# Moving the small resident tiles of a two-layer float32r trunk into a pool of their own that ends on a multiple of 2 KB

## The chip, the cores and the metric

One core of one Trainium2 chip runs the kernel. The time is device microseconds of one execution of the program; several executions are timed, and the median counts. The engines work at the same time: TensorE (PE in the profile, PEld its weight loads), VectorE (DVE), ScalarE (ACT), GpSimd (POOL), SyncE (SP), which here issues all DMAs. The on-chip memory (SBUF) has 128 partitions; a tile takes the same byte addresses in each of them, so a tile's start is one number, in bytes of a partition.

## The reference

A trunk of two layers on 512 tokens of width 1024, all in float32. What matters here is what is multiplied:

```python
def swiglu(x, w_gu, w_down):                 # D_FF = 2816
    gate, up = jnp.split(x @ w_gu, 2, axis=-1)
    return (jax.nn.silu(gate) * up) @ w_down

# layer 0
x = x + 0.5 * swiglu(rms_norm(x, ffn1_norm[0]), ...)
h = rms_norm(x, mix_norm[0]) @ a_w_in[0]     # 6 gated DeltaNet heads, 4 heads over the memory
x = x + concat([o_a, o_m]) @ w_out[0]
x = x + 0.5 * swiglu(rms_norm(x, ffn2_norm[0]), ...)
# one latent K/V from x, shared by the next layer
# layer 1
x = x + 0.5 * swiglu(rms_norm(x, ffn1_norm[1]), ...)
h = rms_norm(x, mix_norm[1]) @ b_w_in[0]     # 6 MLA heads, 4 heads over the memory
x = x + concat([o_b, o_m]) @ w_out[1]
x = x + 0.5 * swiglu(rms_norm(x, ffn2_norm[1]), ...)
return rms_norm(x, final_norm)
```

## The kernel before

**How a product is made.** Activations lie feature-major: a tile of 128 features by 512 tokens. Each float32 operand is split exactly into a part that float32r holds and the remainder: xh and xl for the activations, gh and gl (or dh and dl) for the weights. `mm3` (L196 to L202) then makes three matmuls per 128 features: weights wh against xh (L200), wh against xl (L201), wl against xh (L202). The first operand after the output is the stationary one (128 columns, loaded by PEld), the second is streamed through it, 512 columns of 4 bytes, 2048 bytes of each partition.

**The work.** The four feed-forward parts (`ffn`, calls numbered 0 to 3) take most of the time. Each walks over 22 hidden tiles, two at a time: two tiles of up projection (`gemm`, twice 24 matmuls each: 8 chunks of features, 3 matmuls), whose results are normed, gated and split into hh and hl, and then the down projection (`down`) of the pair before, 8 output tiles of 6 matmuls each. So 96 up-projection matmuls (named mm in the profile, streaming nah, nal and the like, one letter per norm) are followed by 48 down-projection matmuls (dn, streaming hh and hl); at the border a few of the two kinds alternate. In the last pair of the last part (`finish`) the 512 tokens are done in two halves, with 256 columns. Between the parts stand mixer A (the DeltaNet heads in small 128-column float32 matmuls, with the next heads' projections, mm from nbh and nbl, beside them), the latent part, and mixer B. Both end in an output projection (wo, streaming oh and ol, which stand in the tiles of xh and xl). The memory's keys and values (memk, memv) are made inside the first feed-forward part and the latent part.

**What sets the order.** `Weights` loads 1 MB tiles (gr) by SP's queue, and splits them in pieces of 512 columns on ScalarE (L91, the float32r part) and VectorE (L92, the remainder), one to two tiles ahead of their use. The tile scheduler orders each engine's instructions from the program's order. Each engine runs its own list; semaphores join them.

**Where tiles stand.** A pool is one stretch of SBUF. Pools opened one after another follow each other, and in a pool each tag takes its buffers in the order of first use, each rounded up to a multiple of 32 bytes. The first free byte is 16512, which is 128 past a multiple of 2048. The pool `res` comes first, and in it, in this order: cst (the gains and other columns, 128x153, 640 bytes), x0 to x7 (2048 each), ident and ones (512 each), half and warm (32 each), the 16 tiles of xh and xl (2048 each), rcol (two columns of 4, 32 each), the two rows of reciprocal roots (2048 each), memc (32), memr and the memory's keys and values (1024 each), the squares and their sums (2048 each). The pool `wp` of the weight stream follows (gr, gh, gl, two buffers of 8192 bytes each), then the pools of the parts. So the small tiles decide where all later ones begin:

| tiles | start mod 2048 before | after |
|---|---|---|
| x0 to x7 | 768 | 0 |
| xh, xl (also oh, ol) | 1856 | 0 |
| gr, gh, gl | 928 | 1024 |
| feed-forward: g, u, hh, hl, dr, dh, dl | 928 | 1024 |
| latent ch, cl; mixer B's qh, ql | 928 | 1024 |
| memory mh, ml | 928, 1952 | 1024, 0 |
| ident, ones | 768, 1280 | 768, 1280 |

A matmul takes its 128 weight columns at multiples of 512 bytes from the start of gh, gl, dh or dl. Mixer A's own tiles have small ones among them and stand at many different starts, before and after.

The lines that the change and the prediction touch: the pools (L136 to L139), the constants (L180 to L189), `rstd_column` (L229 to L238), `memory_kv` (L373 to L377), `mm3` (L196 to L202), `Weights._split` (L91, L92).

Of the kernel before, what the change touches and what calls it, by code (L numbers as in the profile page):

```python
# [8 lines left out]
F32 = mybir.dt.float32  # L9
# [8 lines left out]
P = 128  # L18
# [17 lines left out]
NCOL = 0  # L36
# [20 lines left out]
class Weights:  # L57
    """A stream of weight tiles in the order of their use: raw loads run two tiles ahead,
    the exact split into a float32r part and the remainder runs one tile ahead."""

# [35 lines left out]
    def start(self, part, parts):  # L96
        """The first tile in parts: their loads, and later their splits by first()."""
        n = self.src[0].shape[1]
        if part == 0:
            t = self.pool.tile([P, self.size], F32, tag=self.tag + "r", bufs=self.raw_bufs,  # L100
                               name=f"{self.tag}r0")
            self.raws.append((t, n))
        c = slice(part * n // parts, (part + 1) * n // parts)
        self.nc.sync.dma_start(self.raws[0][0][:, c], self.src[0][:, c])
# [26 lines left out]
def trunk(ctx, tc, xT, memT, pos, cols, masks, wmem, wgu, wdn, wba, wain, wout, wdkv, wbin,  # L131
          wuqn, wuqr, wukn, wuv, outT, taps=None):
    nc = tc.nc
    taps = taps or {}

    res = ctx.enter_context(tc.tile_pool(name="res", bufs=1))  # L136
    wp = ctx.enter_context(tc.tile_pool(name="wp", bufs=1))
# [5 lines left out]
    def ps(tags, name):  # L143
        """A PSUM bank; "ab" takes the two pairs of banks by turns."""
        k = turn.get(tags, 0)
        turn[tags] = k + 1
        return pp.tile([P, S], F32, tag=tags[k % len(tags)], bufs=2, name=name)
# [31 lines left out]

# [1 line left out]
    cst = res.tile([P, NCOL], F32, name="cst")  # L181
    nc.sync.dma_start(cst, cols)
    x = [res.tile([P, S], F32, tag=f"x{c}", name=f"x{c}") for c in range(KD)]
    ident = res.tile([P, P], F32, name="ident")
    ones = res.tile([P, P], F32, name="ones")
    nc.vector.memset(ones, 1.0)
    half = res.tile([P, 8], F32, name="half")
    nc.vector.memset(half, -0.5)
    nc.scalar.copy(res.tile([P, 8], F32, name="warm"), half)  # L189

# [3 lines left out]

# [1 line left out]
    def mm3(out, ws, xs, first=True, last=True):  # L196
# [20 lines left out]
    def rsqrt(out, src, scale):  # L217
        """(src * scale + eps) ** -0.5 of a few columns."""
        nc.vector.tensor_scalar(out, src, scale, EPS, op0=ALU.mult, op1=ALU.add)
        nc.gpsimd.tensor_tensor(out, out, half[:, :out.shape[1]], op=ALU.pow)  # L220

    def rows_of(c, n, name, tags="d"):
        """Token columns c [128, n] as one row in every partition, in PSUM."""
        p = ps(tags, name)
        for i in range(n):
            nc.tensor.transpose(p[:, i * P:(i + 1) * P], c[:, i:i + 1].broadcast_to([P, P]), ident)
        return p

    def rstd_column(pool, parts, scale, tag, n=NB):  # L229
        """1/rms over the features of parts (squares, feature-major), token-major."""  # L230
        p = ps("d", tag + "ss")
        for i in range(n):
            for j, a in enumerate(parts):
                nc.tensor.matmul(p[:, i:i + 1], a[:, i * P:(i + 1) * P], ones[:, 0:1],
                                 start=j == 0, stop=j == len(parts) - 1)
        c = pool.tile([P, n], F32, tag="rcol", bufs=2, name=tag + "c")
        rsqrt(c, p[:, :n], scale)
        return c  # L238

    def rstd_rows(pool, c, tag, n=NB):  # L240
        """The same in every partition."""
        pr = rows_of(c, n, tag + "row")
        r = pool.tile([P, n * P], F32, tag="rstd", bufs=2, name=tag + "r")
        nc.scalar.copy(r, pr[:, :n * P])
        return r

    class Norm:
        """x * gain split for the tensor engine, chunk by chunk; 1/rms follows once all are in."""

# [103 lines left out]

# [1 line left out]
    memk, memv, memr = [], [], []  # L355

    def memory_kv(l, hook=None):
        with tc.tile_pool(name=f"mem{l}", bufs=1) as mp:
# [14 lines left out]
            if l == 0:  # L373
                c = res.tile([P, 2], F32, name="memc")
                r = res.tile([P, 256], F32, name="memr")
                nc.vector.tensor_copy(c, rstd_column(mp, [acc], 1.0 / 1024, "mem", 2))
                nc.scalar.copy(r, rows_of(c, 2, "memrow")[:, :256])  # L377
                memr.extend((c, r))
            c, r = memr
# [22 lines left out]
    def memory_attention(l, q, pool, out, ts="ab", tt="d", to="c"):  # L402
        """q: two tiles of two heads each, feature-major; out(pair, psum) takes the result."""
        for pr in range(2):
# [43 lines left out]
    def out_begin(os, order, held):  # L448
        """The first four tiles of the output projection without the last operand."""
        for _ in range(2):  # L450
# [21 lines left out]

# [1 line left out]
    def mixer_a(norm, nxt):  # L474
        with ExitStack() as st:
# [25 lines left out]
            def project(h):  # L501
                """q, k, v after their convolutions and the gate, feature-major."""
                o = []
# [24 lines left out]

            # decay and write strength of every head, by rows
            w = G.get()  # L530
# [45 lines left out]
            def prepare(h, q, k, v, gs):  # L576
                """Everything of a head that does not wait for the scan."""
                bb, Gb = t("bb"), t("Gb")
# [3 lines left out]
                cs = [slice(n * P, (n + 1) * P) for n in range(NB)]  # L582
                # decay between tokens, transposed: rows j, columns i
                Dm = t("Dm")
# [7 lines left out]
                nc.scalar.activation(kf, kf, AF.Exp)  # L592
                # lengths of k and q, from their token-major forms; they enter as factors of what
                # the products of the raw k and q are multiplied with
                ss = ap.tile([P, 8], F32, tag="ss", bufs=3, name="ss")
                pkt, pqt = ps("b", "kt"), ps("b", "qt")
                for i, (a, p) in enumerate(((k, pkt), (q, pqt))):
# [6 lines left out]
                    yield  # L604
                # k k^T and k q^T within a block
                pk = ps("b", "kk")
# [16 lines left out]
                nc.vector.tensor_mul(bb, bb, eG)  # L623
                AT = Db  # its upper triangle and diagonal are never read
                nc.vector.tensor_mul(AT, pk, Db)
                # (I + A)^-1: small diagonal blocks by substitution, rows of A brought to every
                # partition of their block
                tmp = t("tmp")
# [45 lines left out]
            def scan(h, AT, xt, QK, kd, vb, qd, kb, fin, rq, gs):  # L674
                cs = [slice(n * P, (n + 1) * P) for n in range(NB)]
                nb = P // SUB
                # the inverse goes on by doubling the size of its blocks; two units by turns
                X, Z = [], []
# [20 lines left out]
                for s in LEVELS:  # L699
# [11 lines left out]
                    for g in range(2):  # L711
                        pr = ps("c", "r")
                        # the last step needs of X the first blocks of 64 only
                        w = 64 if s == LEVELS[-1] else P
# [11 lines left out]
                for g in range(2):  # L726
# [14 lines left out]
                    yield  # L741
                # scan over the blocks, the output token-major
                po = ps("c", "o")
# [54 lines left out]
            def drive(*tasks):  # L798
                """Emit the tasks (a generator and about how many steps it has) side by side, so
                that the products of one fill the waits of the others; return what they return."""  # L800
                done = [0.0] * len(tasks)
# [51 lines left out]

# [1 line left out]
    def rope_tables(cs, sn):  # L855
# [30 lines left out]
    def latent_norm(pool, src, gain, hi, lo):  # L886
        """rms norm over two feature tiles, split for the tensor engine; in two steps."""
        sqs = []
# [27 lines left out]
    def norm_project(norm, w, out):  # L916
        """The first products of a norm, two tiles of features."""
        p0 = gemm(norm, w, 256, 0)
# [5 lines left out]

# [1 line left out]
    def mixer_b(norm, lat, nxt):  # L926
        with ExitStack() as st:
            bp = st.enter_context(tc.tile_pool(name="mixb", bufs=1))

            # tags of the squares of a norm, free meanwhile  # L930
            lent = {"cq": "sq", "qraw": "sq", "qn": "sqa"}
# [86 lines left out]

            # one head begins when the one before it is half done
            tasks = [head(h) for h in range(NH)]  # L1020
# [11 lines left out]

# [1 line left out]
    def gain(name, l=0):  # L1034
# [51 lines left out]
    def finish(ws, hs, pool):  # L1086
        """The last products and the final norm by halves of the tokens, the norm of the first
        half beside the products of the second."""
        acc, rc = [None, None], [None, None]
# [150 lines left out]
```

## Time and profile before

| | us |
|---|---|
| median of three runs | 2081.82 |
| the three runs | 2086.16, 2081.36, 2081.82 |
| span of the profiled execution (first to last instruction) | 2085.2 |
| TensorE busy in the span | 2038.2 |

The profile is of one execution. Its span, 2085.2 us, is the time from its first to its last instruction; the time of a run counts a little more around it (of the three, 2086.16 us lies nearest). Times in the rows are microseconds from the start of the span. Matmuls are pipelined: a row's length is longer than the step to the next row's start, and the steps between starts tell how fast TensorE goes.

### The profile page before, as it was taken

How to read it: one execution, taken by the hardware profiler on the slowest of the kernel's cores; microseconds unless marked ns; L12 is line 12 of the kernel's file. 1: busy time of each engine (PE TensorE's matmuls, PEld its weight loads, DVE VectorE, ACT ScalarE, POOL GpSimd, SP SyncE). 2: the span in 40 equal slices, each digit the busy share in tenths (PEclk: the TensorE clock that was granted, in tenths of full speed). 3: DMA queues.
4: the chain of work that ended last, by engine and by line, in shares of the span. 5: the costliest groups of instructions: out<-in, count | busy, mean ns of one | idle time of the engine just before them, and what ended most of it. 6: DMA issues, size and time to landing. Idle time of an engine off the chain costs nothing.

```text
span 2085.2 us, 24007 instructions
## 1 busy us (share of the span) xinstructions
PE 2038.2 (98%) x9264; PEld 1617.9 (78%) x9264; DVE 1239.3 (59%) x2311; ACT 750.0 (36%) x1566; POOL 118.0 (6%) x85
## 2 busy tenths in 40 slices
PE   8999999989999999999999999999999999999998
PEld 6888888777777678888888888888875588888886
DVE  7655555777777595555547655555557554555555
ACT  6332222565664353222225422222243343222221
POOL 1000000200100020000002000000020020000001
PEclk9999999999999999999999999999999999999999
DMA  6332222332222132322222422222111132222211
GB/s 235 111 118 84 101 82 74 114 112 62 68 91 71 54 125 101 101 84 98 102 71 76 173 101 81 101 93 91 62 39 49 61 124 98 82 100 101 98 44 41
DMA packets 43642, 191.59 MB, mean 92 GB/s; under 512 B 5756, under 2 KB 10108, under 8 KB 28808
## 3 DMA queue, kind: packets, MB, share of 16 engines
q1 hardware_dynamic: 43528, 190.05, 26.6%
q8 instruction: 73, 1.20, 0.2%
q14 instruction: 41, 0.34, 0.0%
HBM read 184.57 MB, written 4.42 MB: 91 GB/s over the span
## 4 chain that ended last, share of the span: by engine, by line
PE 50%; issue 35%; DVE 7%; DMA 3%; ACT 2%; POOL 2%; SPq 0%; DVEq 0%; POOLq 0%; ACTq 0%
PE mm L201 9%; PE mm L202 9%; PE mm L200 9%; PE dn L200 4%; PE dn L201 4%; PE dn L202 4%; DMA ab<-sub 2%; PE wo L200 1%; PE wo L202 1%; PE wo L201 1%; PE sc L995 1%; PE sc L994 1%; DVE gl L92 1%; PE bo L1015 1%; POOL nfsa L269 1%
## 5 line engine op out<-in xcount | busy, mean ns | idle before, releaser
L91 ACT CAST gh<-gr 128x512 fp32r<-128x512 f32 x474 | 261.3, 617 | 380.8 <-PE mm L201 356.1
L92 DVE TENSOR_TENSOR gl<-gr,gh 128x512 fp32r<-128x512 f32 x474 | 314.3, 689 | 15.9 <-ACT gh L91 9.6
L337 DVE SCALAR_TENSOR_TENSOR x<-dn,x 128x512 f32<-128x512 f32 x344 | 236.4, 688 | 89.9 <-PE dn L202 88.3
L200 PE MATMUL dn<-hh,dh 128*128 128x512 f32 (+1 forms) x720 | 278.9, 387 | 1.4 <-DVE x L337 1.0
L202 PE MATMUL dn<-hh,dl 128*128 128x512 f32 (+1 forms) x720 | 277.8, 386 | 0.0
L201 PE MATMUL dn<-hl,dh 128*128 128x512 f32 (+1 forms) x720 | 277.8, 386 | 0.0
L91 ACT CAST dh<-dr 128x512 fp32r<-128x512 f32 x176 | 96.6, 617 | 296.9 <-PE dn L201 284.9
L304 ACT ACTIVATE g<-g 128x512 f32<-128x512 f32 x88 | 55.5, 632 | 323.3 <-DVE g L303 323.2
L200 PEld LDWEIGHTS dn<-hh,dh 128*128 128x128 f32 x720 | 135.3, 188 | 34.9 <-DVE x L337 6.2
L202 PEld LDWEIGHTS dn<-hh,dl 128*128 128x128 f32 x720 | 135.3, 188 | 27.4
L201 PEld LDWEIGHTS dn<-hl,dh 128*128 128x128 f32 x720 | 135.5, 188 | 27.0
L200 PE MATMUL mm<-nah,gh 128*128 128x512 f32 x352 | 140.7, 401 | 6.2 <-ACT gh L116 5.9
L201 PE MATMUL mm<-ncl,gh 128*128 128x512 f32 x352 | 140.3, 399 | 2.0 <-DVE ncl L214 2.0
L201 PE MATMUL mm<-nal,gh 128*128 128x512 f32 x352 | 140.8, 400 | 0.4 <-DVE nal L214 0.4
L202 PE MATMUL mm<-nah,gl 128*128 128x512 f32 x352 | 140.6, 399 | 0.6 <-DVE gl L117 0.6
L200 PE MATMUL mm<-nch,gh 128*128 128x512 f32 x352 | 140.4, 399 | 0.0
L202 PE MATMUL mm<-nch,gl 128*128 128x512 f32 x352 | 140.2, 398 | 0.0
L200 PE MATMUL mm<-ngh,gh 128*128 128x512 f32 x352 | 139.7, 397 | 0.0
L201 PE MATMUL mm<-nel,gh 128*128 128x512 f32 x352 | 139.6, 397 | 0.0
L201 PE MATMUL mm<-ngl,gh 128*128 128x512 f32 x352 | 139.6, 397 | 0.0
L202 PE MATMUL mm<-neh,gl 128*128 128x512 f32 x352 | 139.6, 397 | 0.0
L200 PE MATMUL mm<-neh,gh 128*128 128x512 f32 x352 | 139.6, 396 | 0.0
(414 smaller groups left out, 3566.6 us busy)
## 6 DMA issues: line engine op xcount, KB each, us to landing
gr<-wgu SPq DMA_DIRECT2D x87, 1024.0 KB, 4.8
dr<-wdn SPq DMA_DIRECT2D x88, 512.0 KB, 4.0
gr<-wain SPq DMA_DIRECT2D x13, 1024.0 KB, 4.8
gr<-wout SPq DMA_DIRECT2D x8, 1024.0 KB, 5.9
gr<-wmem SPq DMA_DIRECT2D x4, 1024.0 KB, 4.8
ab<-sub SPq DMA_DIRECT2D x6, 512.0 KB
x<-xT SPq DMA_DIRECT2D x8, 256.0 KB, 6.9
mt<-memT SPq DMA_DIRECT2D x16, 128.0 KB, 2.4
```

Source lines behind the costliest of these rows:

```text
L91: nc.scalar.copy(hi[:, a:b], raw[:, a:b])
L92: nc.vector.tensor_sub(lo[:, a:b], raw[:, a:b], hi[:, a:b].bitcast(F32))
L200: nc.tensor.matmul(out, wh, xh, start=first and k == 0, stop=False)
L201: nc.tensor.matmul(out, wh, xl, start=False, stop=False)
L202: nc.tensor.matmul(out, wl, xh, start=False, stop=last and k == n - 1)
L269: nc.gpsimd.tensor_tensor(acc, self.acc, sq, op=ALU.add)
L304: nc.scalar.activation(g, g, AF.Silu)
L337: nc.vector.scalar_tensor_tensor(x[m], p, 0.5, x[m], op0=ALU.mult, op1=ALU.add)
L994: nc.tensor.matmul(p[:, :nk], qn[:, c], kn[:, :nk], start=True, stop=False)
L995: nc.tensor.matmul(p[:, :nk], qr[h // 2][rows, c], lat["kr"][rows, :nk], start=False, stop=False)
L1015: nc.tensor.matmul(po[:, b * P:], vv[b][:, h * P:(h + 1) * P], pt[:, b, b * P:], start=b == 0, stop=b == NB - 1)
```

## The change

A new pool `small` is opened ahead of `res` and takes cst, ident, ones, half, warm, the columns of reciprocal roots (rcol, from whichever part asks for one) and memc. A tile of 24 zeros (fill, 96 bytes) fills it up: 640 + 512 + 512 + 32 + 32 + 96 + 64 + 32 = 1920 bytes, from 16512 to 18432 = 9 x 2048. In `res` only tiles of 2048 and 1024 bytes remain. The diff without the lines that only delete comments and docstrings:

```diff
+    small = ctx.enter_context(tc.tile_pool(name="small", bufs=1))
     res = ctx.enter_context(tc.tile_pool(name="res", bufs=1))
     wp = ctx.enter_context(tc.tile_pool(name="wp", bufs=1))
...
-    cst = res.tile([P, NCOL], F32, name="cst")
+    cst = small.tile([P, NCOL], F32, name="cst")
     nc.sync.dma_start(cst, cols)
     x = [res.tile([P, S], F32, tag=f"x{c}", name=f"x{c}") for c in range(KD)]
-    ident = res.tile([P, P], F32, name="ident")
-    ones = res.tile([P, P], F32, name="ones")
+    ident = small.tile([P, P], F32, name="ident")
+    ones = small.tile([P, P], F32, name="ones")
     nc.vector.memset(ones, 1.0)
-    half = res.tile([P, 8], F32, name="half")
+    half = small.tile([P, 8], F32, name="half")
     nc.vector.memset(half, -0.5)
-    nc.scalar.copy(res.tile([P, 8], F32, name="warm"), half)
+    nc.scalar.copy(small.tile([P, 8], F32, name="warm"), half)
+    nc.vector.memset(small.tile([P, 24], F32, name="fill"), 0.0)
...
     def rstd_column(pool, parts, scale, tag, n=NB):
...
-        c = pool.tile([P, n], F32, tag="rcol", bufs=2, name=tag + "c")
+        c = small.tile([P, n], F32, tag="rcol", bufs=2, name=tag + "c")
...
             if l == 0:
-                c = res.tile([P, 2], F32, name="memc")
+                c = small.tile([P, 2], F32, name="memc")
```

The order of instructions stays the same on TensorE, ScalarE, GpSimd and SP. On VectorE one is added at the start of the program, where the constants are set and the first chunks of x are split (nal is the remainder of a chunk of x, gl that of the first weight tile). Before:

```order
L186 MEMSET ones 128x128
L188 MEMSET half 128x8
L214 SCALAR_TENSOR_TENSOR nal_101<-x_68,cst,nah_100 128x512
L117 TENSOR_TENSOR gl_105<-gr_84,gh_104 128x512
L214 SCALAR_TENSOR_TENSOR nal_111<-x_69,cst,nah_110 128x512
L214 SCALAR_TENSOR_TENSOR nal_117<-x_70,cst,nah_116 128x512
```

With the change, where lines are numbered two or three higher:

```order
L188 MEMSET ones 128x128
L190 MEMSET half 128x8
L192 MEMSET fill 128x24
L217 SCALAR_TENSOR_TENSOR nal_106<-x_71,cst,nah_105 128x512
L117 TENSOR_TENSOR gl_110<-gr_89,gh_109 128x512
L217 SCALAR_TENSOR_TENSOR nal_116<-x_72,cst,nah_115 128x512
L217 SCALAR_TENSOR_TENSOR nal_122<-x_73,cst,nah_121 128x512
```

The zeros of fill have come in third; all that follows keeps its order.

## Rows read from the trace of the kernel before

**Rows 1.** Page, busy us (share of the span) and instructions of each engine.
```profile
PE 2038.2 (98%) x9264; PEld 1617.9 (78%) x9264; DVE 1239.3 (59%) x2311; ACT 750.0 (36%) x1566; POOL 118.0 (6%) x85
```

**Rows 2.** Windows: us; PE, PEld, DVE, ACT, POOL busy (x instructions); clock, DMA share, GB/s.
```profile
500.00:600.00 100.00, 93.27 (x558) 74.17 (x557) 76.03 (x233) 63.27 (x196) 13.77 (x8) 1.00 0.23 75
900.00:1000.00 100.00, 100.00 (x432) 81.06 (x432) 52.81 (x85) 26.77 (x48) 0.00 (x0) 1.00 0.27 95
2038.50:2050.50 12.00, 12.00 (x53) 9.66 (x52) 2.76 (x4) 1.25 (x2) 0.00 (x0) 1.00 0.00 1
2050.81:2061.47 10.66, 10.66 (x48) 8.83 (x47) 6.74 (x10) 0.62 (x1) 0.00 (x0) 1.00 0.00 0
```

**Rows 3.** Page, chain that ended last, shares by engine.
```profile
PE 50%; issue 35%; DVE 7%; DMA 3%; ACT 2%; POOL 2%; SPq 0%; DVEq 0%; POOLq 0%; ACTq 0%
```

**Rows 4.** Timeline of TensorE (start us, length us): 93 up projections, first and last.
```profile
1209.31 0.40 PE L200 MATMUL mm<-neh,gh 128*128 128x512 f32 x1
...
1230.86 0.40 PE L202 MATMUL mm<-neh,gl 128*128 128x512 f32 x1
```

**Rows 5.** Timeline of TensorE: 48 down projections, then 48 of half width, firsts and lasts.
```profile
2050.81 0.39 PE L200 MATMUL dn<-hh,dh 128*128 128x512 f32 x1
...
2061.47 0.39 PE L202 MATMUL dn<-hh,dl 128*128 128x512 f32 x1
2061.70 0.28 PE L200 MATMUL dn<-hh,dh 128*128 128x256 f32 x1
...
2067.33 0.28 PE L202 MATMUL dn<-hh,dl 128*128 128x256 f32 x1
```

**Rows 6.** Timeline of TensorE: down projections behind two up projections.
```profile
1954.85 0.40 PE L201 MATMUL mm<-ngl,gh 128*128 128x512 f32 x1
1955.08 0.39 PE L202 MATMUL mm<-ngh,gl 128*128 128x512 f32 x1
1955.32 0.40 PE L200 MATMUL dn<-hh,dh 128*128 128x512 f32 x1
...
1957.40 0.39 PE L200 MATMUL dn<-hh,dh 128*128 128x512 f32 x1
```

**Rows 7.** Groups by shape: names, xcount | busy us, mean ns of one | idle before.
```profile
L200 PE MATMUL mm<-nch,gh 128*128 128x512 f32 x352 | 140.4, 399 | 0.0
...
L200 PE MATMUL dn<-hh,dh 128*128 128x512 f32 x688 | 269.8, 392 | 1.4 <-DVE x L337 1.0
...
L200 PE MATMUL mm<-nbh,gh 128*128 128x512 f32 x208 | 87.9, 422 | 0.3 <-DVE cp L517 0.3
...
L200 PE MATMUL wo<-oh,gh 128*128 128x512 f32 x128 | 51.4, 408 | 0.9 <-ACT oh L210 0.8
...
L200 PE MATMUL memk<-mh,gh 128*128 128x256 f32 x32 | 9.3, 291 | 0.0
...
L200 PE MATMUL dn<-hh,dh 128*128 128x256 f32 x32 | 9.1, 285 | 0.0
```

**Rows 8.** Groups by shape, VectorE.
```profile
L92 DVE TENSOR_TENSOR gl<-gr,gh 128x512 fp32r<-128x512 f32 x473 | 313.9, 690 | 15.9 <-ACT gh L91 9.6 <-PE nfrow L226 5.9
...
L337 DVE SCALAR_TENSOR_TENSOR x<-dn,x 128x512 f32<-128x512 f32 x344 | 236.4, 688 | 89.9 <-PE dn L202 88.3
...
L211 DVE TENSOR_TENSOR hl<-u,hh 128x512 fp32r<-128x512 f32 x88 | 60.2, 685 | 3.4 <-ACT hh L210 3.2
```

**Rows 9.** Timeline of VectorE, the first 5 us.
```profile
0.95 0.07 DVE L188 MEMSET half<- 128x8 f32 x1
4.82 0.75 DVE L214 SCALAR_TENSOR_TENSOR nal<-x,cst,nah 128x512 fp32r<-128x512 f32 x1 [3.81 <-ACT nah L213]
```

**Rows 10.** Page, DMA issues: out<-in, count, KB each, median us to landing.
```profile
gr<-wgu SPq DMA_DIRECT2D x87, 1024.0 KB, 4.8
```

**Rows 11.** Timeline of TensorE: mixer A's 24 matmuls with 64 weight columns, first and last.
```profile
395.09 0.39 PE L200 MATMUL mm<-nbh,gh 128*64 128x512 f32 x1
...
400.41 0.39 PE L202 MATMUL mm<-nbh,gl 128*64 128x512 f32 x1
```

## The prediction

> **What bounds the kernel now.** I read the busy times first. TensorE is busy 98% of a span of 2085.2 us, VectorE 59% [rows 1]. [...] The chain that ended last says the same: TensorE's work and its "issue" (waiting for nothing that the profile shows) make up 85% of it, VectorE 7%, DMA 3% [rows 3]. So over four fifths of the kernel the time is the number of matmuls times the spacing of their starts. [...]
>
> **The spacing, by tile.** In the timeline of TensorE, 93 up-projection matmuls in a row start between 1209.31 and 1230.86 us, 92 steps: 21.55 / 92 = 234.2 ns, though each row is 0.40 us long [rows 4]. The last 48 full-width down-projection matmuls start between 2050.81 and 2061.47: 10.66 / 47 = 226.8 ns [rows 5]. Both stream 512 columns of float32r past 128 weight columns. [...] Other traffic does not separate the two kinds: from 2038.5 to 2050.5 us only up projections run, DMA is at 0.00 and VectorE at 23%; from 2050.81 the down projections follow with VectorE at 63%, and they are the faster ones [rows 2].
>
> What differs is the start address of the streamed operand. By the sizes of the tiles, xh and xl begin at 1856 mod 2048, which is 64 mod 128; hh, hl (and ch, qh) begin at 928 mod 2048, which is 32 mod 128, as do all the weights. So the fast kind has stream and weights at the same place mod 512 (416 both), the slow kind has them 96 bytes apart (320 against 416). The output projection streams oh and ol from the tiles of xh and xl; it is on the slow side.
>
> There is also a transient. Where two up-projection matmuls have come between down projections, the nine steps after them, from 1955.32 to 1957.40 us, take 2.08 us, 231 ns each, though all nine stream and load at the down projection's addresses [rows 6]. Such transients follow every mix of the two kinds; spread over all down projections I put them at 1.3 ns, 228.1 on average instead of 226.8 (an estimate: a dozen or so of 48 come about 5 ns late).
>
> **The change, part by part.**
> (1) xh and xl move to 0 mod 2048, weights and feed-forward tiles to 1024 mod 2048. Stream and weights are now at the same place mod 512 everywhere. The nearest measured case with this property is the down projection, so I take its 226.8 ns for every 128x512 float32r matmul.
> Feed-forward up projections: 352 x 3 x 4 = 4224 one group of the twelve, [rows 7], each 234.2 - 226.8 = 7.4 ns: 31.3 us, all on the path, as TensorE has no idle time there [rows 2].
> Down projections: 688 x 3 = 2064 [rows 7], from 228.1 to 226.8: 1.3 x 2064 = 2.7 us.
> Mixers and the latent part: 208 x 3 of mixer A's projection, 24 with 64 weight columns, 128 x 3 of the output projections [rows 7], and 168 in the inputs of the latent part and mixer B (groups like these), together 1200 x 7.4 = 8.9 us. In mixer A TensorE is 93% busy and also waits for VectorE and ScalarE [rows 2], so I count two thirds: 5.9 us; bounds 0 and 8.9.
> Sum: 31.3 + 2.7 + 5.9 = 39.9 us.
> [...] I take 226.8 because it is the only spacing that rows show for the equal-place case.
> (2) VectorE, ScalarE, POOL: the remainders of the weights work on three tiles at 928 mod 2048 (690 ns), the update of x on a tile at 768 and a PSUM bank (688), the remainder of u at 928 (685) [rows 8]. Different starts, one price: I count nothing for moving them, either way; if they changed by 1% they would hide behind TensorE in the feed-forward stretches, where VectorE has 47% to spare.
> (3) The new VectorE instruction, 128x24 zeros: the 128x8 one took 0.07 us at 0.95 us, and VectorE then sits idle for 3.81 us until ScalarE's first result [rows 9]. The zeros fall into that pause. Nothing; if that cover were gone, 0.07 us.
> (4) The two buffers of the reciprocal roots are now shared with the memory part's column, which had its own. The users lie tens of microseconds apart, and the order of instructions is the same on every engine. Nothing.
> (5) DMA: a 1 MB weight tile lands 4.8 us after its issue [rows 10] and one is needed every 11 us of up projection. A start at 1024 instead of 928 can change a little of 4.8; hidden.
> If matmuls come sooner, the next late thing would be VectorE, whose share would go from 53 to 55%. It stays hidden.
>
> The profiled execution spans 2085.2 us and took about 1 us more (2086.16 is the nearest of the three times): 2086.2 - 39.9 = 2046.3. The same 39.9 off the median of 2081.8 gives 2041.9, **2042 us**. With the mixers' bounds and a spacing of 226 to 228 ns the case's own range is 2034 to 2052.
>
> [...]
>
> **The rivals.**
> [...]
> 2. *Slower: a start on a multiple of 64 is the bad one.* The slow kind starts at 0 mod 64, the fast ones at 32 mod 64, and after the change every stream starts at 0 mod 64. Then the up projections stay at 234.2 and the down projections go there: 2064 x 6.1 = 12.6 us, and 312 of half width x 7.5 = 2.4: 2097 us. It counts as slower once the down projections exceed 231 ns (3 x 2064 = 6.2 us, 0.3%). Against it: in [rows 6] matmuls at 32 mod 64 take 231 ns too.
> 3. *No difference*: the surplus hangs on something that comes with xh and xl (sums over 24 matmuls instead of 6; their place low in the memory), and addresses mod 2048 don't matter. 2078 to 2085. [...]
>
> **How the numbers follow.** Forecast 0.42, rival 1 0.30, rival 2 0.13, rival 3 0.15. A measurement of this kernel tells 0.3% (6 us) from nothing, so faster is 0.72, same 0.15, slower 0.13. From 1960 to 2087 lie the forecast, rival 3 and the larger part of rival 1 (0.24): 0.81.
>
> **What would show it.** In the profile after: a run of 92 steps of up projection takes 20.9 us instead of 21.55; 441 matmuls in 100 us instead of 432; no transients after a mix; VectorE rows unchanged at 685 to 690 ns. [...] The forecast is wrong as well if TensorE gains and idle time for VectorE or a lower granted clock eats it.

## The result, and the profile after

The changed kernel takes 2046.32 us (median of four runs, 2043.36 to 2050.37) against 2082.14 us for the kernel before (four runs): a ratio of 0.9821, 95% interval 0.9803 to 0.9839, or 35.8 us less. The prediction was 2042 (1960 to 2087). The profiled execution spans 2045.2 us and took 2047.07; that of before spans 2085.2.

The page of the changed kernel, busy time of each engine, beside [rows 1]:

```profile
PE 1998.0 (98%) x9264; PEld 1612.7 (79%) x9264; DVE 1238.8 (61%) x2312; ACT 749.9 (37%) x1566; POOL 118.3 (6%) x85
```

TensorE still has the same 9264 matmuls and is still busy 98% of the span, but the busy time itself fell by 40.2 us. The other engines do what they did (VectorE 1238.8 against 1239.3 us). So the gain is in the matmuls.

The windows of the changed kernel, the same stretch of 900 to 1000 us as in [rows 2], and the last 48 full-width down projections:

```profile
900.00:1000.00 100.00, 100.00 (x443) 82.71 (x442) 53.12 (x85) 27.38 (x49) 0.00 (x0) 1.00 0.29 99
2010.90:2021.56 10.66, 10.66 (x49) 8.82 (x47) 6.74 (x10) 0.62 (x1) 0.00 (x0) 1.00 0.00 0
```

443 matmuls instead of 432 in 100 us, both at a granted clock of 1.00. The down projections take 10.66 us as before.

The timeline of TensorE in the changed kernel: the same 93 up projections as in [rows 4], first and last.

```profile
1189.03 0.39 PE L203 MATMUL mm<-neh,gh 128*128 128x512 f32 x1
...
1209.88 0.39 PE L205 MATMUL mm<-neh,gl 128*128 128x512 f32 x1
```

20.85 / 92 = 226.6 ns a step, against 234.2. That is the down projection's spacing of [rows 5] (226.8; a hundredth of a microsecond in the starts is 0.1 to 0.2 ns a step).

The same two up projections with ten down projections behind them as in [rows 6], in the changed kernel's timeline:

```profile
1917.40 0.40 PE L205 MATMUL mm<-ngh,gl 128*128 128x512 f32 x1
1917.64 0.40 PE L203 MATMUL dn<-hh,dh 128*128 128x512 f32 x1
...
1919.72 0.39 PE L203 MATMUL dn<-hh,dh 128*128 128x512 f32 x1
```

The nine steps from 1917.64 to 1919.72 take 2.08 us, as before. This transient did not go away. Others did: of 75 places where six or more steps between down projections follow an up projection without a stall, the first six average above 229 ns in 36 before and in 17 with the change.

VectorE's groups by shape and its first two small fills, beside [rows 8] and [rows 9]:

```profile
L92 DVE TENSOR_TENSOR gl<-gr,gh 128x512 fp32r<-128x512 f32 x473 | 314.9, 693 | 15.9 <-ACT gh L91 9.8 <-PE nfrow L229 5.8
L340 DVE SCALAR_TENSOR_TENSOR x<-dn,x 128x512 f32<-128x512 f32 x344 | 236.9, 689 | 89.1 <-PE dn L205 88.0
...
L214 DVE TENSOR_TENSOR hl<-u,hh 128x512 fp32r<-128x512 f32 x88 | 60.7, 689 | 3.1 <-ACT hh L213 2.9
```

```profile
0.95 0.07 DVE L190 MEMSET half<- 128x8 f32 x1
0.97 0.08 DVE L192 MEMSET fill<- 128x24 f32 x1
```

The prices are within 4 ns of those before (690, 688, 685), though all these tiles moved. The new fill of 0.08 us lies in the pause before the first chunk of x.

**Where the 40 us went**, from the starts of each part's first matmul in the two timelines:

| part | before, us | after, us | less |
|---|---|---|---|
| feed-forward part 0, with the memory's keys and values | 389.22 | 381.59 | 7.63 |
| mixer A | 277.10 | 274.04 | 3.06 |
| its output projection, to the start of part 1 | 74.08 | 73.19 | 0.89 |
| feed-forward part 1 | 374.17 | 367.03 | 7.14 |
| latent part | 32.25 | 31.97 | 0.28 |
| feed-forward part 2 | 368.83 | 360.66 | 8.17 |
| mixer B | 131.66 | 128.11 | 3.55 |
| its output projection, to the start of part 3 | 50.48 | 49.23 | 1.25 |
| feed-forward part 3, to the end | 381.55 | 373.34 | 8.21 |

Most of one of these lines is not the change's. In mixer B the two profiles differ by 3.1 us in one place, and there the granted clock differs. Windows of 5 us of the kernel before:

```profile
1615.00:1620.00 5.00, 4.46 (x18) 1.94 (x14) 1.96 (x6) 2.32 (x6) 0.00 (x0) 1.00 0.00 0
1620.00:1625.00 5.00, 5.00 (x13) 2.41 (x13) 1.79 (x6) 0.56 (x2) 0.00 (x0) 0.52 0.00 0
1625.00:1630.00 5.00, 5.00 (x20) 3.60 (x20) 2.37 (x10) 1.42 (x4) 0.00 (x0) 0.80 0.00 0
```

The same place in the changed kernel:

```profile
1588.00:1593.00 5.00, 4.46 (x18) 2.15 (x16) 2.11 (x7) 2.31 (x6) 0.00 (x0) 1.00 0.00 0
1593.00:1598.00 5.00, 5.00 (x20) 2.77 (x20) 3.11 (x13) 1.23 (x4) 0.00 (x0) 1.00 0.00 0
```

In both TensorE idles 0.54 us in the first window; in the profile of before the granted clock is then 0.52 and 0.80 in the next two windows, and in that of the changed kernel it stays at 1.00. The 68 matmuls of this stretch take 21.26 us with the drop and 18.13 to 18.15 without. Of the thirteen profiles of this study four have the drop (before, the two runs below that put pads by part, and the one that starts from the kernel before), nine don't. The up projection steps at 234, 227, 229 to 233 and 227 ns in these four, so the drop goes with no one spacing, and the same 0.54 us of idle time stands in all thirteen. One profile of each kernel can't show whether the drop comes with an execution; but over 27 timed runs of the kernel before, the mean granted clock goes from 0.990 (2089.45 us) to 0.997 (2078.07 us), so something of this kind differs between runs of one kernel. Without it the two profiles are 36.9 us apart, which agrees with the medians' 35.8.

### The profile page after: what moved, and what is told of

It reads as the page before. It is cut to its first block, busy times and chain, and to the rows that moved or that the text cites. A ratio compares the mean times of both kernels' runs of the same rounds, so it can differ in the third digit from the quotient of the medians.

```text
span 2045.2 us, 24008 instructions
## 1 busy us (share of the span) xinstructions
PE 1998.0 (98%) x9264; PEld 1612.7 (79%) x9264; DVE 1238.8 (61%) x2312; ACT 749.9 (37%) x1566; POOL 118.3 (6%) x85
## 4 chain that ended last, share of the span: by engine, by line
PE 50%; issue 36%; DVE 7%; DMA 3%; ACT 2%; POOL 2%; SPq 0%; DVEq 0%; POOLq 0%; ACTq 0%
PE mm L204 9%; PE mm L205 9%; PE mm L203 9%; PE dn L203 4%; PE dn L204 4%; PE dn L205 4%; DMA ab<-sub 2%; PE wo L203 1%; PE wo L205 1%; PE wo L204 1%; PE sc L998 1%; PE sc L997 1%; PE bo L1018 1%; DVE gl L92 1%; POOL nfsa L272 1%
## 5 line engine op out<-in xcount | busy, mean ns | idle before, releaser
L205 PE MATMUL mm<-ngh,gl 128*128 128x512 f32 x352 | 137.0, 389 | 0.0
```

The source lines that it names most:

```text
L205: nc.tensor.matmul(out, wl, xh, start=False, stop=last and k == n - 1)
```

## The experiments

Each kernel but the last is the changed kernel with the edit shown. Each ratio is to the kernel before as timed beside that run (medians from 2081.21 to 2084.36 us). Difference means the start of the streamed operand minus the start of the weights. In all of them a step is the distance of two starts in TensorE's timeline, over the same 93 up projections as above (92 steps) unless the text says otherwise.

**Absolute or relative place: four runs.** The forecast said that stream and weights must stand at the same place; rival 1 said that a misaligned stream pays by itself, whatever the weights do. In the changed kernel both begin at 0 mod 128. The edits move one of the two, by the length of fill and by an idle tile ahead of the weights' pool:

```diff
-    nc.vector.memset(small.tile([P, 24], F32, name="fill"), 0.0)
+    nc.vector.memset(small.tile([P, FILL], F32, name="fill"), 0.0)
+    gap = ctx.enter_context(tc.tile_pool(name="gap", bufs=1))
     wp = ctx.enter_context(tc.tile_pool(name="wp", bufs=1))
+    nc.vector.memset(gap.tile([P, GAP], F32, name="step"), 0.0)
```

FILL, GAP are 24, 8 (weights moved by 32 bytes), 40, 16 (stream by 64, weights by 128), 24, 16 (weights by 64), 32, 24 (stream by 32, weights by 128).

> The stream (xh, xl) stays at 0 mod 128, weights and feed-forward tiles go to 32 mod 128. Three theories, each for the up projection (stream 0, weights 32) and the down projection (32, 32). R, relative place: stream and weights must begin at the same place mod 128: up projection back to 234 ns, down projection 226.8, about 2085 us. S, the stream alone decides (0 and 32 mod 128 cheap, 64 dear): both 226.8 ns, 2046 us. W, weights on a multiple of 64 bytes are cheap with any stream, off it only a stream at the same place is: up projection 234 ns, about 2085 us, as R.

> The stream goes to 64 mod 128, weights and feed-forward tiles stay at 0 mod 128. R, same place mod 128: up projection 234 ns, about 2085 us; if the same place mod 64 is enough, 226.8 ns and 2046 us. S, stream alone: 234 ns, about 2085 us. W, weights on a multiple of 64: 226.8 ns, 2046 us. Down projection (0, 0) 226.8 ns by all.

> The stream stays at 0 mod 128, weights and feed-forward tiles go to 64 mod 128. Up projection (0, 64): R mod 128 234 ns, about 2085 us; R mod 64, S and W 226.8. Down projection (64, 64): R and W 226.8 ns; S 234 ns, which is 2064 x 7 = 14 us more, about 2060 us. So R mod 128 says 2085, S 2060, W and R mod 64 2046.

> The stream goes to 32 mod 128, weights and feed-forward tiles to 0 mod 128. Up projection (32, 0): R, mod 128 or mod 64, 234 ns, about 2085 us; S and W 226.8 ns, 2046 us. Down projection (0, 0) 226.8 ns by all.

Timeline of TensorE, first and last of the 93 up projections, weights moved by 32:

```profile
1203.45 0.40 PE L205 MATMUL mm<-neh,gh 128*128 128x512 f32 x1
...
1224.91 0.40 PE L207 MATMUL mm<-neh,gl 128*128 128x512 f32 x1
```

Stream moved by 64:

```profile
1201.41 0.39 PE L205 MATMUL mm<-neh,gh 128*128 128x512 f32 x1
...
1222.87 0.39 PE L207 MATMUL mm<-neh,gl 128*128 128x512 f32 x1
```

Weights moved by 64, and in the same run the last 48 down projections, whose stream and weights both stand at 64:

```profile
1206.83 0.39 PE L205 MATMUL mm<-neh,gh 128*128 128x512 f32 x1
...
1228.29 0.39 PE L207 MATMUL mm<-neh,gl 128*128 128x512 f32 x1
...
2043.17 0.39 PE L205 MATMUL dn<-hh,dh 128*128 128x512 f32 x1
...
2053.84 0.39 PE L207 MATMUL dn<-hh,dl 128*128 128x512 f32 x1
```

Stream moved by 32:

```profile
1209.95 0.40 PE L205 MATMUL mm<-neh,gh 128*128 128x512 f32 x1
...
1231.50 0.40 PE L207 MATMUL mm<-neh,gl 128*128 128x512 f32 x1
```

| run | stream, weights mod 256 | up projection, ns | us, ratio to before |
|---|---|---|---|
| before | 64, 160 | 234.2 | |
| changed | 0, 0 | 226.6 | 2046.32, 0.9821 [0.9803, 0.9839] |
| weights by 32 | 0, 32 | 21.46 / 92 = 233.3 | 2076.13, 0.9968 [0.9957, 0.9980] |
| stream by 64 | 64, 128 | 21.46 / 92 = 233.3 | 2075.09, 0.9966 [0.9950, 0.9982] |
| weights by 64 | 0, 64 | 21.46 / 92 = 233.3 | 2075.97, 0.9969 [0.9956, 0.9981] |
| stream by 32 | 32, 128 | 21.55 / 92 = 234.2 | 2080.83, 0.9994 [0.9983, 1.0005] |

Whichever of the two is moved, most of the gain goes. The last row has the difference of the kernel before, 160 mod 256, at other addresses, and its spacing to the tenth. The stream at 0 mod 128 is dear in the runs with weights by 32 and by 64, so a well-aligned stream alone brings nothing: rival 1's mechanism is out, and so is the theory S of these runs. At 64 it is dear as an up projection, but as a down projection with weights at 64 it steps 10.67 / 47 = 227.0 ns: rival 2 is out too. W, that weights on a multiple of 64 are cheap, falls with the last three runs. What remains is the relative place, theory R; its 2085 us was 4 to 10 too high, as it put 234 ns on every difference.

**The same place mod what: two runs.** The first puts an idle tile ahead of the down projection's weights, of another length in each feed-forward part (and 256 bytes ahead of the weights' pool); the second shifts hh and hl within longer buffers.

```diff
             def down(b, last):
+                if b == 0:
+                    pad = fp.tile([P, PAD[f]], F32, tag="pad", bufs=1, name="pad")
+                    nc.vector.memset(pad, 0.0)
```

PAD = 32, 64, 8, 24 floats for parts 0 to 3.

```diff
-                hh = fp.tile([P, S], R, tag="hh", bufs=4, name="hh")
+                o = OFF[f]
+                n = S + 32 if o else S
+                hh = fp.tile([P, n], R, tag="hh", bufs=4, name="hh")[:, o:o + S]
```

OFF = 4, 2, 1, 0 floats, and the same for hl.

> Written after the first four runs: up projection 226.8 ns where stream and weights begin at the same place mod 128, 233.3 to 234.2 ns at 32, 64 and 96 apart. Here the stream of the up projection begins 256 bytes apart from its weights (same mod 128 and mod 256, not mod 512); in the four feed-forward parts the down projection's weights stand 128, 256, 32 and 96 bytes behind the place of its stream (mod 512). Theory R128, a difference that is a multiple of 128 costs nothing: up projection 226.8 ns, down projection near 227.4 in parts 0 and 1, 233.3 in part 2 (stream minus weights 96 mod 128, as in the run with weights moved by 32), 234.2 in part 3 (32 mod 128, as in the kernel before); 528 x 6 + 480 x 7 = 6.5 us more than the changed kernel, about 2053. Rival R512, the place mod 512 must be the same: up projection 233 ns or more and parts 0 and 1 too, 4700 x 6.5 + 9.7 more, about 2090.

> Up projection as in the changed kernel (226.8 ns). The streams of the down projection begin 16, 8 and 4 bytes behind the place of their weights mod 128 in feed-forward parts 0, 1 and 2, and at the same place in part 3. If the place counts to the byte: 233 to 234 ns in parts 0 to 2, 227.4 in part 3, 1584 x 6.3 = 10 us more than the changed kernel, about 2056. Rival, only the block of 32 bytes counts in which both begin: 227.4 in all parts, 2046.

Timeline of TensorE in the run with pads, firsts and lasts: rows of 71 down projections at the end of part 0 (128 apart) and of part 1 (256 apart), the 93 up projections (256 apart), and the last 48 down projections of part 3 (160 apart mod 256).

```profile
372.20 0.39 PE L209 MATMUL dn<-hl,dh 128*128 128x512 f32 x1
...
388.47 0.40 PE L210 MATMUL dn<-hh,dl 128*128 128x512 f32 x1
...
1084.83 0.39 PE L209 MATMUL dn<-hl,dh 128*128 128x512 f32 x1
...
1100.76 0.39 PE L210 MATMUL dn<-hh,dl 128*128 128x512 f32 x1
...
1190.35 0.39 PE L208 MATMUL mm<-neh,gh 128*128 128x512 f32 x1
...
1211.21 0.40 PE L210 MATMUL mm<-neh,gl 128*128 128x512 f32 x1
...
2021.38 0.39 PE L208 MATMUL dn<-hh,dh 128*128 128x512 f32 x1
...
2032.39 0.40 PE L210 MATMUL dn<-hh,dl 128*128 128x512 f32 x1
```

A difference of 256 costs nothing: 20.86 / 92 = 226.7 ns in the up projection and 15.93 / 70 = 227.6 in part 1 (the same 71 take 15.95 us, 227.9 ns a step, in the changed kernel). A difference of 128 costs: 16.27 / 70 = 232.4. Part 2 (224 apart) has 233.3, part 3 11.01 / 47 = 234.3, which is the kernel before's up projection on other tiles. Neither R128 nor R512 holds; the modulus is 256. The time, 2058.51 us (ratio 0.9898 [0.9881, 0.9915]), is 5 above R128's 2053. That part 0 pays as well accounts for 528 x 5 ns = 2.6 of them.

The run with shifts of bytes took 2060.41 us (0.9900 [0.9884, 0.9917]): 230.7 ns in part 0, 235.0 in part 1 (8 bytes), 236.7 in part 2 (4 bytes) and 226.6 in part 3 (none). It is flawed by what the other run found: buffers of 2176 bytes bring differences of 128 into parts 0 to 2 along with the shift. But 235.0 and 236.7 are more than 128 costs by itself, so even 4 bytes are not free, and the rival of 32-byte blocks is out. The rows can also be taken apart: of the two hidden tiles of a pair one has the shift alone and the other 128 more. Between two matmuls that both have the shift alone the mean step is 230.9 ns (16 bytes), 234.9 (8 bytes) and 235.6 (4 bytes).

**Within a row of three: two runs.** The weights' remainders, then the stream's, were put 64 bytes from all else, to see whether a matmul pays for its own weights or for those loaded beside it.

```diff
-            lo = self.pool.tile([P, self.size], R, tag=self.tag + "l", bufs=self.bufs,
-                                name=f"{self.tag}l{k}")
+            lo = self.pool.tile([P, self.size + 32], R, tag=self.tag + "l", bufs=self.bufs,
+                                name=f"{self.tag}l{k}")[:, 16:16 + self.size]
```

```diff
-            lo = res.tile([P, S], R, tag=f"xl{c}", name=f"{self.tag}l{c}")
+            o = 16 if c < 7 else 0
+            lo = res.tile([P, S + 2 * o], R, tag=f"xl{c}", name=f"{self.tag}l{c}")[:, o:o + S]
```

> Only the remainders of the weights (gl, dl; the third matmul of each three) stand 64 bytes apart from all else mod 128. If the difference of a matmul's stream to its own weights is paid: the step from the third matmul to the next 233.3 ns, the other two 226.8. If the difference to the weights that are loaded while it streams (the next matmul's) is paid: the step from the second to the third 233.3. Either way a third of some 7000 matmuls pay 6.5 ns: 15 us more than the changed kernel, about 2061. Rival, matmuls settle to one spacing only in an undisturbed row: all three steps 230 ns or more, 23 us more or above, about 2070 to 2090.

> Only the remainders of the stream xl of seven of the eight chunks (the second matmul of each three of the up projection) begin 64 bytes apart mod 128; the eighth chunk, the output projections and the down projection have no difference. If each matmul pays for its own stream: the step from the second to the third matmul 233.3 ns, the others 226.8; 4224 / 3 x 7/8 x 6.5 = 8 us more, about 2054, and the same step whether own or next weights count. Rival, settling to one spacing only in an undisturbed row: all three steps 230 ns or more, 14 us more or above, about 2060 to 2075.

They took 2074.92 us (0.9970 [0.9960, 0.9980]) and 2069.99 us (0.9948 [0.9933, 0.9963]); the 92 steps are 231.1 and 231.5 ns on average. Both times are the rivals' (all three steps pay). But neither edit gives one difference alone. In the first, buffers 128 bytes longer put the third matmul's difference at 192 and 64 mod 256 in turns; the first two matmuls stay at 0, and yet step at 229.2 and 230.1 ns in feed-forward part 2, against 234.3 for the third. In the second, buffers of 2176 bytes bring in differences of 128, as with the bytes. So the first was made once more, cleanly.

**The rest of the circle, the clean repeat, and the smallest edit.** The last three runs. The first has GAP 48 (the up projection 64 apart) and PAD 56, 0, 40, 32 (down projections 32, 96 and 128 apart in parts 0, 2, 3), and shifts hh and hl by 16 bytes in part 1, in buffers 256 bytes longer. The second repeats the weights' remainders for gl alone with `self.size + 64`. The third starts from the kernel before and leaves out the change altogether but for one idle tile:

```diff
+    gap = ctx.enter_context(tc.tile_pool(name="gap", bufs=1))
     wp = ctx.enter_context(tc.tile_pool(name="wp", bufs=1))
...
+    nc.vector.memset(gap.tile([P, 40], F32, name="step"), 0.0)
```

> Written after the first eight runs, with differences as stream minus weights mod 256: 0 costs 226.8 ns, 128, 160, 192 and 224 cost 232.6 to 234.2. Here the rest: up projection 64, down projection 32 in feed-forward part 0, 96 in part 2, 128 in part 3; in part 1 it is 16 bytes, this time with buffers 256 bytes longer, so that no difference of 128 comes in. Theory R256, only a multiple of 256 is cheap: up projection about 233.3 ns (as 192), parts 0, 2, 3 233 to 234, part 1 231 or more; 4224 x 6.5 + 800 x 6.5 + 2064 x 6 = 45 us more than the changed kernel, about 2090. Rival, what counts is only whether the stream lies on the far side of its weights (differences of 32 to 96 cheap, 128 to 224 dear): up projection 226.8 ns, part 3 233, 480 x 6 = 3 us more, about 2049.

> The run with the weights' remainders 64 bytes apart again, for gl alone and with buffers 256 bytes longer, so that no difference of 128 comes in: the third matmul of each three of the up projection has stream minus weights 192 mod 256, the first two 0; the down projection stays at 0 (227.5 ns). If each matmul pays for its own weights: third step 233.3 ns, the others 226.8; 4224 / 3 x 6.5 + 2 = 11 us more than the changed kernel, about 2057. If it pays for the weights loaded beside it: the same, on the second step. Rival, a change of the difference within the row unsettles the two matmuls behind it as well: all three steps average 230 ns or more, 4224 x 3.5 + 3 = 18 us more or above, about 2064 to 2075.

> The kernel before with one idle tile of 160 bytes between the resident tiles and the weight stream, and nothing else of the change: streams stay at 1856 mod 2048, weights and feed-forward tiles go to 1088; both are 64 mod 256, none begins on a multiple of 128. Theory R256: all difference 0, up projection 226.8 ns, as fast as the changed kernel, 2046 us (ratio 0.982 to before). Rival, the multiples of 1 and 2 KB themselves bring a part: up projection above 228 ns, 2052 us or more (ratio above 0.985).

Timeline of the run with the rest of the differences: a row of up projections of part 0 (64 apart), the 71 down projections of part 0 (32 apart) and of part 1 (16 apart), then the up projections of part 2 (64 apart).

```profile
182.57 0.40 PE L208 MATMUL mm<-nah,gh 128*128 128x512 f32 x1
...
204.04 0.40 PE L210 MATMUL mm<-nah,gl 128*128 128x512 f32 x1
...
377.11 0.39 PE L209 MATMUL dn<-hl,dh 128*128 128x512 f32 x1
...
393.44 0.39 PE L210 MATMUL dn<-hh,dl 128*128 128x512 f32 x1
...
1094.02 0.40 PE L209 MATMUL dn<-hl,dh 128*128 128x512 f32 x1
...
1110.23 0.39 PE L210 MATMUL dn<-hh,dl 128*128 128x512 f32 x1
...
1201.05 0.39 PE L208 MATMUL mm<-neh,gh 128*128 128x512 f32 x1
...
1222.12 0.39 PE L210 MATMUL mm<-neh,gl 128*128 128x512 f32 x1
```

All of the circle, in ns a step from rows of 36 steps or more:

| difference mod 256 | 0 | 16 | 32 | 64 | 96 | 128 | 160 | 192 | 224 |
|---|---|---|---|---|---|---|---|---|---|
| ns | 226.7 | 231.6 | 233.3 | 229.0 or 233.3 | 233.3 | 232.4 | 234.2 | 233.3 | 233.3 |

Only 0 has the low spacing. The run took 2070.81 us (0.9933 [0.9917, 0.9950]), between R256's 2090 and the rival's 2049. R256 was too dear on one point: a difference of 64 costs 229.0 in these 92 steps (21.07 / 92; in such a row the three steps of a row of three are about 232, 226 and 229 ns). It does not do so everywhere: of the 40 rows of 93 or more up projections, 32 step at 229 to 230 ns and eight, seven in part 0 and the first of part 2, at 233.3 (21.47 / 92 = 233.4 in the row above), the spacing of its mirror image 192. So at 64 the difference alone does not fix the spacing; what picks one of the two stays open. The rival's cheap side is out, with 233.3 at 32 (16.33 / 70) and at 96. A difference of 16 bytes costs too: 16.21 / 70 = 231.6 ns.

The clean repeat took 2066.77 us (0.9914 [0.9900, 0.9929]). In feed-forward part 2 the step behind each of the three matmuls is 228.5 ns (weights wh, stream xh), 229.1 (wh, xl) and 235.7 (wl, xh), 693.3 together against 3 x 226.7 = 680.1. So the third, whose own weights stand apart, pays most, but the row of three pays 13.2 ns, twice 6.6. The forecasts of one dear step in three (2057) fall; the rival's 2064 to 2075 held the time. That two of three matmuls are concerned (the one whose own weights stand apart, and the one beside which these are loaded) fits this sum, and isn't shown by it.

The smallest edit took 2049.26 us, ratio 0.9832 [0.9817, 0.9846]; the changed kernel has 0.9821 [0.9803, 0.9839]. Its timeline, 93 up projections and the last 48 down projections:

```profile
1188.96 0.39 PE L202 MATMUL mm<-neh,gh 128*128 128x512 f32 x1
...
1209.82 0.39 PE L204 MATMUL mm<-neh,gl 128*128 128x512 f32 x1
...
2014.00 0.39 PE L202 MATMUL dn<-hh,dh 128*128 128x512 f32 x1
...
2024.65 0.39 PE L204 MATMUL dn<-hh,dl 128*128 128x512 f32 x1
```

20.86 / 92 = 226.7 and 10.65 / 47 = 226.6 ns, with streams and weights at 64 mod 256 and nothing that matters on a multiple of 2 KB, 1 KB or even 128 bytes. Its profile spans 2048.4 us and has the clock drop of mixer B (granted clock 0.51 from 1595 to 1600 us); less those 3.1 us that is 2045.3, against the changed kernel's 2045.2. So neither the multiples of 2 KB nor the shared columns bring or cost anything that these runs can tell: the difference of 0 mod 256 is the whole change, as far as the two overlapping intervals can tell. Why the difference counts, and what in TensorE or its reads it touches, no run here shows.

## Why the prediction was right, and where it was off

**The cause and the spacing** were right. The step that carried the forecast, that equal places give the down projection's 226.8 ns, came out at 226.6; 92 steps were to take 20.9 us and take 20.85. The prediction said the same place mod 512; the runs show mod 256, which holds here as well.

**The 36 to 37 us that the change saved, against 39.9.** By the parts: the mixers, their output projections and the latent part gave 3.06 + 0.89 + 0.28 + 3.55 + 1.25 = 9.0, less 3.1 for the clock 5.9, against a term of 5.9. That this agrees to the tenth is luck: the two thirds in it were a guess between bounds of 0 and 8.9. The feed-forward parts gave 7.63 + 7.14 + 8.17 + 8.21 = 31.2 against 31.3 + 2.7 = 34.0. Two steps fell short there.

The first is the term of 2.7 us for the transients, and the sign "no transients after a mix". They were taken to come from the mix of the two kinds' addresses, but with equal addresses those of [rows 6] are still there. Over all steps between neighbouring down projections without a stall the mean went from 228.1 to 227.5 ns only: about 0.63 x 2064 = 1.3 us. So about half of the term went with the mixed addresses. What makes the rest stays open; in both kernels such slow steps also follow places where TensorE had stalled between two down projections. Of those with three or more steps behind them before the next stall, these average above 229 ns in 11 of 12 before and in 13 of 13 with the change; in the rows of 70 steps the first ten average 229 to 231 ns and the other sixty 227.2 to 227.3.

The second is "all on the path, as TensorE has no idle time there". It has some at the start of part 1. Windows of the first 16 us of part 1 before, and after:

```profile
746.30:762.30 16.00, 14.02 (x58) 10.52 (x56) 15.76 (x23) 7.86 (x15) 6.31 (x2) 0.89 0.37 141
```

```profile
734.90:750.90 16.00, 13.24 (x53) 9.91 (x51) 15.76 (x23) 7.90 (x14) 6.31 (x2) 0.89 0.43 161
```

TensorE's longest wait in them, before and after:

```profile
748.64 0.51 PE L201 MATMUL mm<-ncl,gh 128*128 128x512 f32 x1 [1.98 <-DVE ncl L214]
```

```profile
738.00 0.50 PE L204 MATMUL mm<-ncl,gh 128*128 128x512 f32 x1 [2.72 <-DVE ncl L217]
```

VectorE is 15.76 of 16 us busy in both, splitting the chunks of x and the weights and making the rotary tables, and TensorE waits for it. A TensorE that comes sooner waits longer, 2.72 us instead of 1.98, and so gives back most of the 0.89 us of the output projection just before: 53 matmuls in these 16 us where there were 58. At its 57th matmul part 1 is 0.6 us behind the kernel before, where 56 x 7.4 ns should have put it 0.4 ahead. In part 0 the 60th matmul starts 21.91 us after the first instead of 22.06: 0.15 us where 59 x 7.4 ns are 0.44, as between the two TensorE waits 1.2 us for first operands before and 1.4 after. Together that is some 1.3 us of the 31.3.

The sum was taken off the profiled 2086.2 and off the median, which lie 4.4 us apart. Of these 4.4, 3.1 have a place in the trace: the clock drop in mixer B, in this one execution. So it is luck that 2086.2 - 39.9 gives the measured 2046.3: a base that is 3.1 us too high meets a saving that is some 3 us too large.

One reading of the rows carried no term and does not hold: that 64 weight columns instead of 128 take off 3 ns, 5.32 / 23 = 231.3 [rows 11] against 234.2 [rows 4]. In the run with the stream moved by 32, whose difference is 160 as well, the same 24 matmuls step at 233.5 ns, and the 128-column ones at 234.2.

**The parts that were costed at nothing** cost nothing: VectorE's rows are at 689 to 693 ns, fill takes 0.08 us in the pause, and the smallest edit, without the shared columns, has the same time within the intervals.

**The rivals.** Rival 1, a misaligned stream that pays by itself, needed steps well below the down projection's 226.8 ns. That there are such steps was the author's estimate; the 0.24 that the chance of the range takes from this rival, and the range's lower end, 1960, stand on it. No run shows one: no row's average is below 226.6 ns. Rival 2 (slower) needed the down projections to go to 234 ns; they stayed at 10.66 / 47 = 226.8. Rival 3, by which the up projection's extra 7.4 ns hang on something else than addresses, fell with the first 92 steps: 226.6.

## What to carry to other kernels

Where matmuls of one kind step some nanoseconds slower than another kind of the same shape, compare the start addresses of the streamed operand and of the weights: here float32r matmuls of 128x512 with 128 weight columns step at 226.7 ns in an undisturbed row when the two begin at the same place mod 256, and at 229 to 237 otherwise, wherever the pair stands. One idle tile of the right length between two pools is enough (160 bytes here: 226.7 ns), and one of the wrong length undoes it (32 bytes ahead of the weights' pool: 233.3). Count steps between starts over a long row: the lengths of the rows (0.39 and 0.40 us) hardly show it.

## What the runs showed that was not expected

The cost is not monotonic in the difference: 64 costs 2.3 ns in most rows and its mirror image 192 6.6 in all; 4 and 8 bytes cost more (235.6 and 234.9, where both neighbours have the shift alone) than any whole multiple of 32. Equal places cost the same in undisturbed rows, wherever the two stood: 226.6 ns at 0 mod 128 (changed kernel), 226.8 at 32 (down projection before), 226.6 to 227.0 at 64 (smallest edit; weights by 64). The two widths of [rows 5] show a part that does not shrink with the columns: 5.63 / 47 = 119.8 ns for 256 of them, so 2 x 119.8 - 226.8 = 12.8 ns a matmul, an estimate from these two rows (13.2 in the changed kernel, where the 48 of half width step at 5.64 / 47 = 120.0). It is not a matter of these differences, as all these rows have equal places.

The rule was read from matmuls with 128 weight columns. The 24 of [rows 11], with 64, come to the same place mod 256 too, but step at 5.29 / 23 = 230.0 ns in the changed kernel, after 231.3:

```profile
387.65 0.40 PE L203 MATMUL mm<-nbh,gh 128*64 128x512 f32 x1
...
392.94 0.40 PE L205 MATMUL mm<-nbh,gl 128*64 128x512 f32 x1
```

In the clean repeat, where every third of them stands 192 apart, they take 227.2 ns. What holds for them these runs don't show.

TensorE's granted clock fell in mixer B in four of thirteen profiles (to 0.52 over 5 us in that of before), and the 68 matmuls there took 3.1 us more; the 0.54 us of idle time ahead of them stands in all thirteen. Two profiles of the same instructions can differ by that much in one place that the edit did not touch; a table by parts finds it, a comparison of two spans does not.
